# A rotary embedding on one core: how slab 0 is loaded, and how some loads and stores are cut into DMAs

## The chip, the cores and the metric

The kernel runs on one core of one Trainium2 chip. The metric is the device time of one execution in microseconds (us); several executions are timed and the median is given. One further execution is taken with the hardware profiler, and all views below come from it.

## What is computed

`x` is a float32 tensor of 16 batches, 512 positions and 1024 numbers (16 heads of 64). `cos` and `sin` have one row of 32 numbers for each position. In each head, the first 32 numbers x1 and the last 32 numbers x2 are turned against each other:

```python
x1, x2 = x[..., :half_dim], x[..., half_dim:]
rotated = np.concatenate([x1 * cos - x2 * sin,
                          x1 * sin + x2 * cos], axis=-1)
```

The output has the size of `x`: 33.55 MB are read and as many written, with very little arithmetic on each number.

## The kernel before

**Tiling.** The input is taken as 8 slabs of two batches (`nslabs` = 8), 4 MB each: 128 partitions with 8 positions each (`rpp` = 8), so 8192 numbers or 32 KB in a partition. Two slabs make a pair. The two slabs of a pair lie side by side in memory for each partition (line 60), so a DMA of one slab moves rows of 32 KB and a DMA of a pair moves rows of 64 KB. There are three tiles for pairs in the core's memory (line 52, `places`); the fourth pair (slabs 6 and 7) takes the place of the first.

**Loads and stores.** `load(s, n, parts)` and `store(s, n, parts)` (lines 68 to 73) move n slabs from slab s on, on the partitions `parts`. Both go through `issue` (line 65) on SP's DMA queue, in the order of the program. `EVEN` and `ODD` (line 76) are every second partition. The order on SP is: load 0 (line 79), load 1 (line 94), load 2-3 in an EVEN and an ODD part (lines 95 and 96), load 4-5 (line 97); then store 0-1 and load 6-7, each in an EVEN and an ODD part, when slab 1 is done (lines 174 to 177); store 2-3 as one DMA when slab 3 is done, store 4-5 in an EVEN and an ODD part when slab 5 is done, store 6-7 as one DMA when slab 7 is done (lines 178 to 180). Load 6-7 EVEN waits for store 0-1 EVEN, and the ODD part for the ODD part, since they use the same memory.

**ScalarE's queue** has three DMAs at the start: the two tables cos and sin (line 89, 64 partitions with 1 KB each), and a short write of a zeroed tile `blank` (128 numbers, 512 bytes, lines 82 and 83) to the first bytes of the output (line 91). Store 0-1 later overwrites these bytes.

**The tables.** GpSimd casts the tables to bf16 (line 112), TensorE spreads them over the 128 partitions by matmuls against a tile of ones and minus ones (line 119), and VectorE (table 0, line 126) and ScalarE (table 1, line 159) copy them out.

**The work on a slab.** It goes in passes: slab 0 in two passes of 4 positions, slab 7 in passes of 4, 2 and 2, all others in one (line 134). For each pass ScalarE casts the float32 slab to bf16 into the lower half of its own memory (`cast`, line 147), VectorE multiplies twice by a table (line 167) and adds (line 170), and ScalarE copies the result out as float32 over the slab (line 173). All ScalarE copies go through line 151, in the order of the program. In the round of slab s, ScalarE first casts slab s+1 (lines 161 to 164) and then copies slab s out, so a slab's copy-out, and the store behind it, stand behind the landing of the next slab.

**Semaphores.** The framework gives each DMA one of eight completion semaphores in turn. The ninth DMA takes the one of the first, and its issue waits until the first has landed.

Of the kernel before, what the change touches and what calls it, by code (L numbers as in the profile page):

```python
# [2 lines left out]

# [4 lines left out]


@with_exitstack  # L10
def kernel(
    ctx: ExitStack,
    tc: tile.TileContext,
    x: bass.AP,
    cos: bass.AP,
    sin: bass.AP,
    num_heads: int,
    out: bass.AP,
):
    nc = tc.nc  # L20
    P = nc.NUM_PARTITIONS

    batch, seq, dim = x.shape
    nh = num_heads
    hd = dim // nh
    half = hd // 2
    bf16 = mybir.dt.bfloat16
    f32 = mybir.dt.float32

    nb = 2  # L30
    nslabs = batch // nb
    rpp = nb * seq // P
    W = rpp * dim
    TP = seq // rpp
    TW = rpp * half

    out_flat = out.rearrange("b s h d -> b s (h d)")

    singles = ctx.enter_context(tc.tile_pool(name="singles", bufs=1))
    pairs = ctx.enter_context(tc.tile_pool(name="pairs", bufs=3))  # L40
    psum = ctx.enter_context(tc.tile_pool(
        name="psum", bufs=1, space=bass.MemoryType.PSUM))


    def view(t, offset, *dims):
        return dataclasses.replace(t, offset=t.offset + offset,
                                   ap=[t.ap[0], *[list(d) for d in dims]])

    places = [pairs.tile([P, 2 * W], f32, tag="pair", name="pair") for _ in range(3)]


    def here(s, n=1):
        return view(places[s // 2 % 3], s % 2 * W, (1, n * W))


    def there(t, s, n=1):
        return bass.AP(tensor=t.tensor, offset=t.offset + s // 2 * 2 * P * W + s % 2 * W,  # L60
                       ap=[[2 * W, P], [1, n * W]])


    def issue(out, in_):
        tc.keep_in_program_order(nc.sync.dma_start(out=out, in_=in_))  # L65


    def load(s, n=1, parts=slice(None)):
        issue(here(s, n)[parts], there(x, s, n)[parts])


    def store(s, n=1, parts=slice(None)):
        issue(there(out_flat, s, n)[parts], here(s, n)[parts])


    EVEN, ODD = slice(0, P, 2), slice(1, P, 2)


    load(0)


    blank = singles.tile([1, P], f32, tag="blank")
    nc.vector.memset(blank, 0.0)  # L83


    cos_sb = singles.tile([TP, TW], f32, tag="cos_sb")
    sin_sb = singles.tile([TP, TW], f32, tag="sin_sb")
    for t, src in ((cos_sb, cos), (sin_sb, sin)):
        tc.keep_in_program_order(nc.scalar.dma_start(out=t, in_=bass.AP(
            tensor=src.tensor, offset=src.offset, ap=[[TW, TP], [1, TW]])))  # L90
    tc.keep_in_program_order(nc.scalar.dma_start(out=bass.AP(
        tensor=out_flat.tensor, offset=out_flat.offset, ap=[[P, 1], [1, P]]), in_=blank))

    load(1)
    for parts in (EVEN, ODD):
        load(2, 2, parts)
    load(4, 2)


    pick = singles.tile([TP, 4 * P], bf16, tag="pick")  # L100
    nc.gpsimd.memset(pick, 0.0)  # L101
    for h in range(2):
        for g in range(2):
            part = view(pick, (2 * h + g) * P, (TP // 2, 2 * P // TP), (1, TP // 2))
            nc.gpsimd.affine_select(  # L105
                out=part, in_=part, compare_op=mybir.AluOpType.not_equal,
                fill=1.0 - 2.0 * g, base=-h, pattern=[[0, 2 * P // TP], [-2, TP // 2]],
                channel_multiplier=1)

    tab1 = singles.tile([TP, 2 * TW], bf16, tag="tab1")  # L110
    for i, t in enumerate((cos_sb, sin_sb)):
        nc.gpsimd.tensor_copy(out=view(tab1, i * TW, (1, TW)), in_=t)  # L112

    accs, tabs = [], []
    for h in range(2):
        acc = psum.tile([P, 2 * rpp * hd], f32, tag=f"acc{h}", name="acc")
        for i in range(2):
            for f in range(2):
                nc.tensor.matmul(  # L119
                    view(acc, i * rpp * hd + f * half, (hd, rpp), (1, half)),  # L120
                    view(pick, (2 * h + i * f) * P, (1, P)),
                    view(tab1, i * TW, (half, rpp), (1, half)),
                    start=True, stop=True)
        accs.append(acc)
        tabs.append(singles.tile([P, 2 * rpp * hd], bf16, tag=f"tab{h}", name="tab"))
    nc.vector.tensor_copy(out=tabs[0], in_=accs[0])  # L126

    passes = []
    for s in range(nslabs):
        r = 0
        for n in {0: (4, 4), nslabs - 1: (4, 2, 2)}.get(s, (rpp,)):
            passes.append((s, r, n))
            r += n


    def halves(u):
        s, r, n = u  # L140
        t = here(s).bitcast(bf16)
        return [view(t, (2 * r + i * n) * dim, (1, n * dim)) for i in range(2)]


    def cast(u):
        s, r, n = u
        copy(halves(u)[0], view(here(s), r * dim, (1, n * dim)))


    def copy(out, in_):  # L150
        tc.keep_in_program_order(nc.scalar.copy(out=out, in_=in_))  # L151


    for i, u in enumerate(passes):
        s, r, n = u
        if i == 0:
            cast(u)
            cast(passes[1])
            copy(tabs[1], accs[1])
            cast(passes[2])  # L160
        elif s > 0:
            for v in passes:
                if v[0] == s + 1:
                    cast(v)
        lo, up = halves(u)
        for t, a in ((up, 0), (lo, rpp * hd)):
            nc.vector.tensor_mul(  # L167
                out=t, in0=lo,
                in1=view(tabs[s % 2], a + r * hd, (hd, n), (0, nh), (1, hd)))
        nc.vector.tensor_add(  # L170
            out=up, in0=up, in1=view(lo, half, (hd, n * nh), (-half, 2), (1, half)))

        copy(view(here(s), r * dim, (1, n * dim)), up)
        if s == 1:
            for act in (store, load):
                for parts in (EVEN, ODD):
                    act(0 if act is store else 6, 2, parts)
        elif s % 2 and r + n == rpp:
            for parts in (EVEN, ODD) if s == 5 else (slice(None),):
                store(s - 1, 2, parts)  # L180


# [1 line left out]
_INS = ['x', 'cos', 'sin', 'num_heads']  # L184
_OUTS = [((16, 512, 16, 64), 'float32')]

_NUMBERS = {'num_heads': 16}


# [26 lines left out]
```

## Time and profile before

| what | us |
|---|---|
| median of 3 executions (161.56 to 162.01) | 161.57 |
| the profiled execution | 161.8 |
| its span, from first to last instruction | 160.0 |
| ScalarE (ACT) busy | 114.0 |
| VectorE (DVE) busy | 108.0 |
| GpSimd (POOL) busy | 2.6 |
| TensorE (PE) busy | 2.0 |

All times in the views are counted from the first instruction of the span. These moments of the profiled execution come up later. They are landings of DMAs and the times at which SP issues a DMA:

| event | at us |
|---|---|
| SP issues load 0 | 0.74 |
| cos lands, sin lands | 10.84, 16.11 |
| load 0 lands, first cast on ScalarE | 13.59, 13.61 |
| first multiply on VectorE | 18.56 |
| load 1 lands | 23.40 |
| load 2-3 has landed (the ODD part) | 42.75 |
| SP issues store 0-1 | 56.80 |
| load 4-5 lands | 62.23 |
| load 6-7 has landed | 101.02 |
| SP issues store 6-7 | 137.66 |
| store 6-7 lands | 159.19 |

A group of instructions in the profile is given by line, engine, operation and tile; "<-DMA pair<-in_x_dram" behind an idle time says what ended it. "q1" is SP's DMA queue and "q10" ScalarE's. One DMA is cut into packets, here one for each partition's row, and these are shared out over 16 DMA engines; each engine also writes a record of 4 bytes when its part of a DMA is complete.

### The profile page before, as it was taken

What the parts mean: (1) busy time and instruction counts of PE and PEld (TensorE: products, weight loads), DVE (VectorE), ACT (ScalarE), POOL (GpSimd) and SP (SyncE); (2) the same over time, 40 slices, a digit from 0 to 9 for tenths busy, and PEclk for the clock granted to TensorE, in tenths of its full rate; (3) what the DMA queues carried; (4) which work ended last, traced back from release to release, by engine and by line L of the source; (5) the groups of instructions that cost most, each with busy time, mean ns of one, the idle gap of its engine ahead of it and who ended that gap; (6) DMA issues with size and microseconds to landing.
All of it is one profiled execution on the core that took longest, in us unless ns stands there. A gap on an engine that the chain in (4) does not pass through costs nothing.

```text
span 160.0 us, 176 instructions
## 1 busy us (share of the span) xinstructions
PE 2.0 (1%) x8; PEld 1.0 (1%) x8; DVE 108.0 (68%) x35; ACT 114.0 (71%) x24; POOL 2.6 (2%) x11
## 2 busy tenths in 40 slices
PE   0010300000000000000000000000000000000000
PEld 0000100000000000000000000000000000000000
DVE  0000699999935998999899899919999997000000
ACT  3005959993299999999999995799999969400000
POOL 4000000000000000000000000000000000000000
DMA  7999999699699699897996996996996996996991
GB/s 262 405 401 405 393 524 524 262 524 524 262 524 524 262 524 410 377 524 344 442 524 278 508 524 278 508 524 262 524 524 262 524 491 295 524 491 295 524 459 66
DMA packets 1522, 67.24 MB, mean 420 GB/s; under 512 B 241, under 2 KB 370, under 8 KB 370
## 3 DMA queue, kind: packets, MB, share of 16 engines
q1 hardware_dynamic: 1360, 67.11, 97.7%
q10 hardware_dynamic: 162, 0.13, 0.3%
HBM read 33.69 MB, written 33.55 MB: 420 GB/s over the span
## 4 chain that ended last, share of the span: by engine, by line
DMA 53%; DVE 14%; ACT 12%; issue 5%; ACTq 2%; SPq 1%
DMA pair<-in_x_dram 37%; DMA out_dram<-pair 15%; ACT pair L151 12%; DVE pair L167 10%; DVE pair L170 4%; ACTq L211 1%; SPq L65 1%; ACTq L151 0%
## 5 line engine op out<-in xcount | busy, mean ns | idle before, releaser
L151 ACT CAST pair<-pair 128x8192 bf16<-128x8192 f32 (+5 forms) x22 | 111.8, 5153 | 20.9 <-DMA pair<-in_x_dram 19.5
L167 DVE TENSOR_TENSOR pair<-pair,tab 128x8192 bf16<-128x8192 bf16 (+2 forms) x22 | 71.4, 3259 | 9.8 <-ACT pair L151 9.4
L170 DVE TENSOR_TENSOR pair<-pair 128x8192 bf16<-128x8192 bf16 (+2 forms) x11 | 35.8, 3259 | 0.3
L126 DVE CAST tab<-acc 128x1024 bf16<-128x1024 f32 x1 | 1.2, 1225 | 16.2 <-PE acc L119 16.2
L151 ACT ACT_TABLE_LOAD x1 | 1.3, 1283 | 2.8 <-issue 2.8
L119 PE MATMUL acc<-tab,pick 64*128 64x256 bf16 x8 | 2.0, 405 | 16.0 <-POOL tab L112 16.0
L119 PEld LDWEIGHTS <-pick 64*128 64x128 bf16 x8 | 1.0, 130 | 16.5 <-issue 14.5
L105 POOL TENSOR_SCALAR_AFFINE_SELECT pick<-pick 64x128 bf16<-64x128 bf16 x4 | 1.1, 302 | 0.1
L151 ACT CAST tab<-acc 128x1024 bf16<-128x1024 f32 x1 | 1.0, 1003 | 0.0
L83 DVE MEMSET blank<- 1x128 f32 x1 | 0.2, 165 | 0.8 <-PEq L197 0.8
L112 POOL CAST tab<-cos_sb 64x256 bf16<-64x256 f32 x1 | 0.4, 389 | 8.5 <-DMA cos_sb<-in_cos_dram 8.5
L101 POOL MEMSET pick<- 64x512 bf16 x1 | 0.5, 517 | 0.3 <-POOLq L197 0.3
L112 POOL CAST tab<-sin_sb 64x256 bf16<-64x256 f32 x1 | 0.4, 394 | 4.9 <-DMA sin_sb<-in_sin_dram 4.9
L197 POOL MEMSET const-float32-0.0<- 128x1 f32 x1 | 0.1, 103 | 0.2 <-issue 0.2
L197 POOL MEMSET const-bfloat16-1.0<- 128x1 bf16 x1 | 0.1, 106 | 0.0
L197 POOL MEMSET const-uint8-127<- 128x1 uint8 x1 | 0.1, 106 | 0.0
L197 POOL MEMSET const-float32-1.0<- 128x1 f32 x1 | 0.1, 103 | 0.0
## 6 DMA issues: line engine op xcount, KB each, us to landing
pair<-in_x_dram SPq DMA_DIRECT2D x2, 4096.0 KB, 17.5
out_dram<-pair SPq DMA_DIRECT2D x6, 22.8
pair<-in_x_dram SPq DMA_DIRECT2D x5, 36.0
cos_sb<-in_cos_dram ACTq DMA_DIRECT2D x1, 64.0 KB, 10.1
sin_sb<-in_sin_dram ACTq DMA_DIRECT2D x1, 64.0 KB, 14.8
out_dram<-blank ACTq DMA_DIRECT2D x1, 0.5 KB
```

The lines of the kernel that those rows point to most:

```text
L65: tc.keep_in_program_order(nc.sync.dma_start(out=out, in_=in_))
L83: nc.vector.memset(blank, 0.0)
L101: nc.gpsimd.memset(pick, 0.0)
L105: nc.gpsimd.affine_select(out=part, in_=part, compare_op=mybir.AluOpType.not_equal, fill=1.0 - 2.0 * g, base=-h, pattern=[[0, 2 * P // TP] ...
L112: nc.gpsimd.tensor_copy(out=view(tab1, i * TW, (1, TW)), in_=t)
L119: nc.tensor.matmul(view(acc, i * rpp * hd + f * half, (hd, rpp), (1, half)), view(pick, (2 * h + i * f) * P, (1, P)), view(tab1, i * TW, ( ...
L126: nc.vector.tensor_copy(out=tabs[0], in_=accs[0])
L151: tc.keep_in_program_order(nc.scalar.copy(out=out, in_=in_))
L167: nc.vector.tensor_mul(out=t, in0=lo, in1=view(tabs[s % 2], a + r * hd, (hd, n), (0, nh), (1, hd)))
L170: nc.vector.tensor_add(out=up, in0=up, in1=view(lo, half, (hd, n * nh), (-half, 2), (1, half)))
L197: nc = _bacc.Bacc("TRN2", target_bir_lowering=False, num_devices=1)
L211: with _tile.TileContext(nc) as tc:
```

## The change

Slab 0 is loaded by four DMAs, the k-th of which takes the partitions k, k+4, k+8 and so on (32 partitions each). The `blank` tile, its memset and its write to the output are gone. Load 2-3 and store 4-5 are one DMA over all partitions instead of an EVEN and an ODD part. Store 0-1 and load 6-7 stay cut in two.

```diff
-    load(0)
-
-
-    blank = singles.tile([1, P], f32, tag="blank")
-    nc.vector.memset(blank, 0.0)
+    for k in range(4):
+        load(0, 1, slice(k, P, 4))
...
-    tc.keep_in_program_order(nc.scalar.dma_start(out=bass.AP(
-        tensor=out_flat.tensor, offset=out_flat.offset, ap=[[P, 1], [1, P]]), in_=blank))
 
     load(1)
-    for parts in (EVEN, ODD):
-        load(2, 2, parts)
+    load(2, 2)
     load(4, 2)
...
         elif s % 2 and r + n == rpp:
-            for parts in (EVEN, ODD) if s == 5 else (slice(None),):
-                store(s - 1, 2, parts)
+            store(s - 1, 2)
```

In the compiled program the number of DMAs on SP stays 13. Two waits stand elsewhere than before. SP's issue of load 4-5, now the ninth DMA, waits for the first one by the order of the semaphores, which is cos. And ScalarE's waits for slab 0, now four, are spread over two instructions: three of them stand on the load of the activation table, which is the instruction ahead of the first cast, and one on the cast.

## The prediction

> **What bounds the kernel now.** I read the page from its DMA rows first, because two engines are busy only some 70% of the span and neither leads. These are lines of the page: the span, the DMA rows of the 40 slices, and the load queue.
>
> ```profile
> span 160.0 us, 176 instructions
> ...
> DMA  7999999699699699897996996996996996996991
> GB/s 262 405 401 405 393 524 524 262 524 524 262 524 524 262 524 410 377 524 344 442 524 278 508 524 278 508 524 262 524 524 262 524 491 295 524 491 295 524 459 66
> ...
> q1 hardware_dynamic: 1360, 67.11, 97.7%
> ```
>
> The 16 engines spend 97.7% of the span on SP's queue. The dips to 262 GB/s look like idling, but each stands beside 524: a slice is 4 us, and long packets are counted where they begin. Stretches cut at the landings (the view of busy time in windows; the last two columns are DMA share and GB/s) even this out:
>
> ```profile
> 0.00:2.00 2.00, 0.00 (x0) 0.10 (x1) 0.17 (x1) 0.00 (x0) 1.40 (x8) 1.00 0.68 197
> 2.00:23.40 21.40, 2.02 (x8) 0.94 (x7) 6.04 (x4) 9.30 (x4) 1.19 (x4) 1.00 1.03 429
> 23.40:61.50 38.10, 0.00 (x0) 0.00 (x0) 33.41 (x10) 32.70 (x6) 0.00 (x0) 1.00 0.97 420
> 61.50:81.00 19.50, 0.00 (x0) 0.00 (x0) 18.43 (x5) 19.50 (x4) 0.00 (x0) 1.00 1.06 457
> 81.00:100.50 19.50, 0.00 (x0) 0.00 (x0) 18.87 (x6) 17.29 (x3) 0.00 (x0) 1.00 1.01 437
> 100.50:139.00 38.50, 0.00 (x0) 0.00 (x0) 31.12 (x13) 35.17 (x9) 0.00 (x0) 1.00 0.99 427
> 139.00:160.00 21.00, 0.00 (x0) 0.00 (x0) 0.00 (x0) 0.00 (x0) 0.00 (x0) 1.00 0.86 371
> ```
>
> No stretch between 2.0 and 139 us is below 0.97. The trace also holds a record of every DMA packet (queue, start, duration, size), and these say it sharply: each engine moves 16 packets of 32 KB and 56 of 64 KB. A 64 KB packet takes 2.418 us, a 32 KB packet 1.213, each starting as the last ends. So the packets alone need 16 x 1.213 + 56 x 2.418 = 154.8 us; the first starts at 1.76 us and the last ends at 158.85, 157.1 us later. The loss is 2.3 us in all: 0.53 because the first packet of an engine takes 1.74 (median), 0.45 in the nine packets after about 8 us, some 0.5 where a store follows a load or the last store begins, the rest in 162 short packets, in how far the engines start apart (1.76 to 2.31) and in how far they end apart (157.96 to 158.85). **The queue is never empty.** Only what shortens or lengthens this row of packets, or lets it run dry, moves the end.
>
> Does it nearly run dry? The waits of SP's queue and the longest waits of the compute engines:
>
> ```profile
> SPq L65 <- ACT pair L151: 91.5, 4, 38.5
> SPq L65 <- DMA out_dram<-pair: 23.4, 2, 13.9
> ...
> SPq L65 <- DMA out_dram<-blank: 4.6, 1, 4.6
> ```
>
> ```profile
> 42.83 20.86 ACT L151 CAST pair<-pair 128x8192 bf16<-128x8192 f32 x3 [5.37 <-DMA pair<-in_x_dram]
> ```
>
> SP issues a store when ScalarE's last copy of a pair is done. By the packet records the queue had work until 61.3 when store 0-1 was issued at 56.8, until 119.3 when store 4-5 was issued at 116.8, and until 138.6 (first engine) to 139.3 (last) when store 6-7 was issued at 137.66. Issue to first packet is at most 1.0 us there, so the slack is about 3.5, 1.5 and 0 to 0.7 us. The last two count from slab 6-7's landing at 101.02: chain and queue both hang on it and shift together, so a shift of the whole row keeps this slack.
>
> **The change, part by part.** All against the profiled execution: 161.8 us, of which 160.0 is the span and 1.8 lies around it; the median of the runs is 161.57, 0.23 lower.
>
> 1. *Slab 0 in four DMAs.* Bytes, row length (32 KB) and packet count are the same: 32 partitions over 16 engines, two packets each, four times. Three more completion records per engine at 9 ns each: +0.03 us. SP issues four instead of one; the issues of this line took 0.39 to 0.60 us, so the fourth is out near 2.5 us, when each engine is still on the first two packets (3.0 us of work from 1.76). Not starved. Does a stride of 4 cost? No trace shows it; the nearest row is a stride of 2: the EVEN and ODD loads of slabs 2-3 took 2.42 us per packet, like load 4-5 over all partitions. I take 0. Bounds: below, the short list may reach the late engines earlier (they start up to 0.55 after the first) and spare the slow first packet (0.53), together -1.1; above, +1.6 (rival C).
>
> 2. *Tables land earlier.* The engine takes a packet of SP's queue and one of ScalarE's in turn. Now cos has five turns (four packets of 46 ns and the completion) and sin five more, each behind a 1.21 us packet, so they land at 10.84 and 16.11. Afterwards the quarters' completions take turns of 9 ns, so cos ends after the fourth x packet instead of the sixth and sin after the eighth instead of the tenth: about 8.2 and 13.2 us. It would let VectorE's first multiply (18.56 now, 2.45 after sin) start at 15.7.
>
> ```profile
> 13.61 7.11 ACT L151 CAST pair<-pair 128x4096 bf16<-128x4096 f32 x2 [9.55 <-DMA pair<-in_x_dram]
> 16.17 0.39 POOL L112 CAST tab<-sin_sb 64x256 bf16<-64x256 f32 x1 [4.89 <-DMA sin_sb<-in_sin_dram]
> ```
>
> But it needs ScalarE's first cast too, and that moves the other way. In the changed program the waits for three quarters hang on the activation table load ahead of that cast, the last quarter's among them. That load (1.28 us, from 2.78 now) then runs at about 13.7 to 15.0, and the first cast from 15.0 to 18.6, as late as VectorE starts today. Queued behind it on ScalarE: the second cast (3.6) and the copy of table 1 (1.0), done at 23.1, still before slab 1 lands (23.4; 1.79 us of idle time there now pays for the 1.28). Sum 0. If this cover were gone, VectorE's idle 4.5 us ahead of 49.88, waiting for slabs 2-3 (42.75), hides up to 4.5 us more. An earlier multiply is worth nothing for the same reason.
>
> 3. *Load 4-5 waits.* The changed program makes SP wait for the cos DMA before it issues load 4-5 (it is the ninth DMA, and reuses that one's semaphore). Behind it on SP stands store 0-1, due at 56.8. Load 4-5 goes out near 8.2 us instead of 3; the queue has work till 41.9. Cost 0, cover 33 us.
>
> 4. *Load 2-3 and store 4-5 whole.* One issue (about 0.5 us of SP) and one completion record per engine less each: -0.02 us. ScalarE waits for both halves of slabs 2-3 today anyway; packets of half and whole stores both take 2.418 us. Cost 0; bounds 0.3 both ways from the 0.1 to 0.34 us by which single packets at a change from load to store are longer.
>
> 5. *No short write.* It goes with VectorE's memset (0.17), one issue on ScalarE (0.79, in its idle time), a 27 ns packet with its completion on one engine, and the 4.6 us that SP waits for its landing, which lie inside the wait for 56.8. Gain 0.04 at most. Above: +0.5 (rival D).
>
> Sum: +0.03 - 0.02 - 0.04, and about -0.1 for a slightly earlier and closer start: 161.8 - 0.1 = 161.7 profiled, 161.5 beside the median.
>
> **The rivals.**
>
> B, *the start gains more*: short lists start all 16 engines together and the slow first packet shrinks. For: the last three engines start 0.1 us after one another. Against: engines that start late today finish their first packet in 1.47 to 1.64 instead of 1.8 to 2.0, so that the starts' spread of 0.55 is already 0.47 at its end, and the four engines that end last are not these three. 0.5 to 1.1 less: about 160.8.
>
> C, *each quarter starts cold* (the other side): the second to fourth quarter pays the 0.53 us of a first packet again, 3 x 0.53 = +1.6, 163.1. It decides once a quarter's first packet is over 0.16 us (a third of 0.48) longer than 1.213, since nothing behind slab 0 gives time back. Against: load 1 follows load 0 in the same queue with 1.3 us packets amid sin's, and loads 2-3 follow with no step at all. [...]
>
> D, *the short write warms the path to the output*: without it the first store's packets pay what the first load's did, +0.5, 162.1. For: all first store packets take 2.418 us today, with no slow first one. Against: it ran on one engine of 16, and the other 15 are as fast.
>
> E, *the change does more than the row of packets shows*, through the earlier tables: excluded up to 4.5 us by VectorE's wait, so it has no share of its own.
>
> **How the numbers follow.** About 0.3% (0.48 us) is what a measurement here can tell from no change. Forecast, no change, 161.5 (161.1 to 162.0): 0.72, of which 0.03 passes the bound on either side. B 0.13, C 0.07, D 0.08, half of it past the bound. Faster 0.13 + 0.03 = 0.16; slower 0.07 + 0.04 + 0.03 = 0.14; same 0.70. The range 160.9 to 162.1 takes in the forecast, about half of B and most of D.
>
> **What would show it.** Right: x packets at 1.21 and 2.42 us with no gap; cos landing near 8.2 and sin near 13.2; the table load at 13.7 and the first multiply within 0.5 us of 18.56; store 0-1 issued near 56.8 and store 6-7 near 137.6; 97 to 98% on q1. Wrong: 32 KB packets well over 1.3 us in the quarters (C); the first packets of the first store over 2.5 us (D); a last store issued over 1 us after the queue ran dry; or slabs 2-3 landing before 42.3 (B).

## The result and the profile after

| | before | changed |
|---|---|---|
| median of 22 runs each, us | 161.88 (161.47 to 162.37) | 162.24 (161.84 to 162.63) |
| ratio to before | 1 | 1.0020 (95%: 1.0011 to 1.0030) |
| profiled execution, its span, us | 161.8, 160.0 | 162.38, 160.6 |

The change costs 0.36 us. That is inside the 0.3% that was named as the bound of "no change", but it has the other sign than the forecast, and 162.24 lies above the range that ended at 162.1. Of the 0.74 us between the forecast and this median, 0.31 belong to the yardstick: the three runs of the kernel before had a median of 161.57, the 22 runs of it beside the changed kernel 161.88. The same 0.36 us on top of 161.57 would have been 161.93, inside the range. So three runs were too few to forecast a time to 0.3 us, and that much of the miss is bad luck; the sign of the change is not.

One correction to the section on the change: SP issues 14 DMAs in the changed kernel, not 13. With the tables (and the short write, before) there are 16 in all in both kernels. This number comes up again.

The page of the changed kernel, the lines that answer to those of before:

```profile
span 160.6 us, 176 instructions
...
DMA  5999999699699697996996996997998998989974
GB/s 171 399 458 441 392 522 522 261 522 522 261 522 506 278 522 310 473 522 261 522 522 261 522 522 261 522 441 343 522 424 359 522 424 359 522 375 408 522 343 180
...
q1 hardware_dynamic: 1376, 67.11, 97.5%
```

The queue is as full as before (97.5% against 97.7%). What differs is the first digit: 5 instead of 7. The windows at the start say the same (the last columns are DMA share and GB/s):

```profile
0.00:2.00 2.00, 0.00 (x0) 0.10 (x1) 0.00 (x0) 0.00 (x0) 1.41 (x8) 1.00 0.00 0
2.00:23.40 21.40, 2.02 (x8) 0.93 (x7) 5.61 (x3) 9.30 (x4) 1.18 (x4) 1.00 1.08 447
```

In the first 2 us, where the kernel before had a share of 0.68, no packet has begun. The chain of the first microseconds shows what SP does there (start, duration), first before, then changed:

```profile
0.74 0.39 SPq L65
1.13 0.05 issue
1.18 0.42 SPq L65
1.61 0.04 issue
1.65 0.57 SPq L65
```

```profile
0.73 0.55 SPq L65
1.28 0.06 issue
1.34 0.58 SPq L65
```

These issues of a DMA over all partitions take 0.39 to 0.42 us, those of every fourth partition 0.55 to 0.58. A DMA that takes every second or every fourth partition is called stepped below. The second issue ends at 1.60 before and at 1.91 now. By the packet records the first packet begins 0.16 us after that in both: at 1.76 and at 2.08. The 0.57 in the chain of before is the EVEN part of load 2-3, and a whole load 2-3 took 0.42 at the same place (kernels 3 and 7 below): the price of a stepped issue stood in the view of before. From the fourth issue on the step no longer tells: load 4-5, over all partitions, took 0.60 before.

Then the timeline of slab 0 in the changed kernel:

```profile
11.59 0.39 POOL L106 CAST tab<-sin_sb 64x256 bf16<-64x256 f32 x1 [4.62 <-DMA sin_sb<-in_sin_dram]
...
14.05 1.28 ACT L145 ACT_TABLE_LOAD   x1 [14.05 <-DMA pair<-in_x_dram]
15.34 7.11 ACT L145 CAST pair<-pair 128x4096 bf16<-128x4096 f32 x2
18.98 6.82 DVE L161 TENSOR_TENSOR pair<-pair,tab 128x4096 bf16<-128x4096 bf16 x3 [5.10 <-ACT pair L145]
```

The tables land at 6.52 and 11.53 (before: 10.84 and 16.11), the table load waits for slab 0, and VectorE starts 0.42 us later than before, now waiting for ScalarE. Nothing follows from that: VectorE still idles 4.31 us ahead of slab 2. Store 0-1 is issued at 57.00 (56.80), store 6-7 at 138.30 (137.69 by its record; 137.66 in the table of before).

### The profile page after: what moved, and what is told of

Its sections match the earlier page's. It is cut to its first block, busy times and chain, and to the rows that moved or that the text cites. A ratio compares the mean times of both kernels' runs of the same rounds, so it can differ in the third digit from the quotient of the medians.

```text
span 160.6 us, 176 instructions
## 1 busy us (share of the span) xinstructions
PE 2.0 (1%) x8; PEld 1.0 (1%) x8; DVE 107.9 (67%) x34; ACT 114.0 (71%) x24; POOL 2.6 (2%) x11
## 3 DMA queue, kind: packets, MB, share of 16 engines
q1 hardware_dynamic: 1376, 67.11, 97.5%
## 4 chain that ended last, share of the span: by engine, by line
DMA 52%; DVE 14%; ACT 12%; issue 5%; SPq 2%; ACTq 2%
DMA pair<-in_x_dram 36%; DMA out_dram<-pair 15%; ACT pair L145 12%; DVE pair L161 10%; DVE pair L164 4%; SPq L65 2%; ACTq L204 1%; ACTq L145 0%
```

## How the experiments were read

Packet records carry most of what follows, so here is one table of all profiles. "DMAs" counts those of both queues. "First" is the start of the first x packet; "load 1" the mean over the 16 engines of the end of its last packet; "joint" the mean duration of the last packets of load 4-5, those just ahead of the first store (2.418 without a joint); "last" the mean end of the last packets; "tail" the time from the last landing to the end of the span. Several values are several profiles of one kernel.

| kernel | DMAs | first | load 1 | joint | last | tail | ratio to before (95%) |
|---|---|---|---|---|---|---|---|
| before | 16 | 1.76, 1.76 | 22.73, 22.79 | 2.58, 2.67 | 158.31, 158.57 | 0.83, 0.83 | |
| load 1 late | 16 | 1.76 | 22.71 | 2.62 | 158.37 | 0.83 | |
| tables late | 16 | 1.75 | 22.77 | 2.61 | 158.32 | 0.83 | 1.0000 (0.9988 to 1.0012) |
| write on 16 engines | 16 | 1.76 | 22.75 | 2.60 | 158.33 | 0.83 | 1.0009 (1.0000 to 1.0017) |
| no write | 15 | 1.75 | 22.69 | 2.65 | 158.32 | 0.90 | 1.0007 (0.9997 to 1.0017) |
| 2-3, 4-5 whole | 14 | 1.76 | 22.68 | 2.86 | 158.73 | 0.96 | 1.0006 (0.9998 to 1.0014) |
| store 0-1, load 6-7 whole | 14 | 1.76 | 22.75 | 2.85 | 162.05 | 0.96 | (one run) |
| changed, slab 0 whole | 13 | 1.74, 1.74 | 22.97, 22.78 | 2.43, 2.75 | 158.46, 158.46 | 1.02, 1.02 | 1.0021 (1.0011 to 1.0031), 1.0012 (1.0001 to 1.0023) |
| changed | 16 | 2.08, 2.06, 2.07 | 22.93, 22.99, 23.09 | 2.86, 2.84, 2.53 | 159.06, 158.87, 158.63 | 0.83, 0.83, 0.83 | 1.0020 (1.0011 to 1.0030), 1.0017 (1.0007 to 1.0027) |
| changed, with write | 17 | 2.06 | 23.03 | 2.66 | 158.61 | 0.93 | 1.0028 (1.0017 to 1.0039) |
| halves | 17 | 2.34 | 22.94 | 3.08 | 159.18 | 0.94 | 1.0041 (1.0026 to 1.0056) |
| quarters, 2-3 whole | 18 | 2.35 | 22.92 | 3.00 | 158.91 | 1.00 | 1.0051 (1.0035 to 1.0067) |
| quarters, no write | 18 | 2.35, 2.35 | 22.97, 22.95 | 3.31, 2.97 | 159.27, 158.87 | 1.00, 1.00 | 1.0052 (1.0038 to 1.0066) |
| quarters alone | 19 | 2.35 | 23.01 | 3.17 | 159.16 | 1.06 | 1.0064 (1.0040 to 1.0088) |
| blocks | 16 | 1.77 | 32.51 | 2.42 | 167.96 | 0.83 | 1.0592 (1.0578 to 1.0606) |

The theory after the result was: the loss has two places, the start (stepped issues) and the joint ahead of the first store (the missing short write). Its rivals: one of the two alone, the cuts of load 2-3 and store 4-5, or scatter.

## The experiments

**1. Quarters alone.**

```diff
-    load(0)
+    for k in range(4):
+        load(0, 1, slice(k, P, 4))
```

> The kernel before with slab 0 alone cut into four DMAs. Theory (two places: the start pays for the cut, the first store pays for the missing short write): first packets start near 2.08 us instead of 1.76, load 1 lands about 0.25 later (23.65), the last packets of load 4-5 stay at a median of 2.55 us as before, and the end is 0.2 to 0.3 us later than before. Rival (the start costs nothing in the end, all of the loss is at the first store): the same landing of load 1 shift, but the end within 0.1 us of before. Second rival (the longer packets at the first store come from the cut of slab 0): last packets of load 4-5 near 2.9 us, end +0.4 to +0.6.

162.66 against 161.81, 0.85 us: more than the whole change (one of the eight runs took 164.21, hence the wide interval). The first packets are at 2.35 and the joint is 3.17, longer even than the second rival had it; the theory, with 2.08 and 2.55, is wrong in both. Against the means of four profiles (16 names them), this one has lost 0.26 us at the end of load 1, 0.55 in the joint and 0.23 in the tail; 16 says what the tail is.

**2. No short write.**

```diff
-    blank = singles.tile([1, P], f32, tag="blank")
-    nc.vector.memset(blank, 0.0)
...
-    tc.keep_in_program_order(nc.scalar.dma_start(out=bass.AP(
-        tensor=out_flat.tensor, offset=out_flat.offset, ap=[[P, 1], [1, P]]), in_=blank))
```

> The kernel before without the short write and its tile. Theory: the first packets start at 1.76 us and load 1 lands at 23.4 as before; the last packets of load 4-5, those before the first store, take a median of 2.9 us instead of 2.55 and the end is 0.2 to 0.4 us later. Rival (these packets scatter from execution to execution or depend on how loads and stores are cut): 2.5 to 2.6 us, end within 0.1 us of before.

Joint 2.65, 161.85 against 161.81: the rival. Leaving out the write shows nowhere; the first store's packets take 2.418 us here too.

**3. Load 2-3 and store 4-5 whole.**

```diff
-    for parts in (EVEN, ODD):
-        load(2, 2, parts)
+    load(2, 2)
...
-            for parts in (EVEN, ODD) if s == 5 else (slice(None),):
-                store(s - 1, 2, parts)
+            store(s - 1, 2)
```

> The kernel before with load 2-3 and store 4-5 as one DMA each. Theory: no change, end within 0.1 us of before, and the last packets of load 4-5 at 2.5 to 2.6 us. Rival (the cut of load 2-3 sets how the first store begins): last packets of load 4-5 near 2.9 us and the end 0.2 to 0.4 us later. A rise at the last store alone (its first packets over 2.45 us) would come from store 4-5 being whole, worth at most 0.1.

161.81 against 161.81, ratio 1.0006 with 1 in its interval. The joint was 2.86 in the one profile, as the rival had it, and that execution took 162.21, the longest of the 12; the median did not follow. So a long joint can belong to one execution and not to the kernel.

**4. The write on all 16 engines.**

```diff
-    blank = singles.tile([1, P], f32, tag="blank")
+    blank = singles.tile([16, P], f32, tag="blank")
...
-        tensor=out_flat.tensor, offset=out_flat.offset, ap=[[P, 1], [1, P]]), in_=blank))
+        tensor=out_flat.tensor, offset=out_flat.offset, ap=[[P, 16], [1, P]]), in_=blank))
```

> The kernel before with the short write widened from 1 row of 512 bytes to 16 rows, one for each of the 16 DMA engines. Theory (a first write to the output costs something on each engine, which the short write takes on itself where it runs): the last packets of load 4-5 fall from a median of 2.55 us toward 2.42 and the end is 0.05 to 0.3 us earlier. Rival (one early write does all there is to do, or the write does nothing): packets stay at 2.5 to 2.6 us, end within 0.1 us of before.

Joint 2.60, 162.02 against 161.81: nothing gained. A first write on every engine did not shorten the joint, against the theory of a warmed path.

**5. Quarters without the write, load 2-3 and store 4-5 still cut** (the edits of 1 and 2).

> The kernel before with slab 0 in four DMAs and without the short write; load 2-3 and store 4-5 stay cut. The quarters alone cost 0.85 us with the short write in place (medians 162.66 and 161.81), and 0.36 in the whole change. Theory (two queues that issue at once hold each other up: ScalarE's short write at 2 us delays the lists of the quarters): without it first packets near 2.08 us and the end 0.3 to 0.4 us later than before. Rival (the uncut load 2-3 is what saves the rest): first packets near 2.35 as in the quarters alone, end 0.7 to 0.9 later.

162.56 against 161.75, first packets at 2.35: the rival, the write holds up nothing.

**6. The changed kernel with the write.**

```diff
+    blank = singles.tile([1, P], f32, tag="blank")
+    nc.vector.memset(blank, 0.0)
...
+    tc.keep_in_program_order(nc.scalar.dma_start(out=bass.AP(
+        tensor=out_flat.tensor, offset=out_flat.offset, ap=[[P, 1], [1, P]]), in_=blank))
```

> The changed kernel with the short write put back. Theory (the short write delays the quarters): first packets near 2.35 us and the end 0.7 to 0.9 us later than before. Rival (load 2-3 uncut saves the rest): first packets near 2.08 us, end 0.3 to 0.4 later.

First packets at 2.06, 162.20 against 161.75 (0.45): the rival again, a little beyond its 0.4. That it is load 2-3 that saves the rest is not shown by this; 14 tests it.

**7. The changed kernel with slab 0 whole.**

```diff
-    for k in range(4):
-        load(0, 1, slice(k, P, 4))
+    load(0)
```

> The changed kernel with slab 0 in one DMA again. Theory (all of the loss is from the quarters): first packets at 1.76 us, load 1 landing at 23.4, end within 0.15 us of before. Rival (leaving out the write or the cuts costs by itself): end 0.2 to 0.4 us later, with the last packets of load 4-5 at 2.9 us.

162.10 against 161.75 (0.35), though the first packets are at 1.74 and the joint is gone (2.43): neither. Load 1 ended at 22.97, as late as with quarters. By this the quarters would cost nothing; 16 takes it up.

**8. Blocks.**

```diff
-        load(0, 1, slice(k, P, 4))
+        load(0, 1, slice(32 * k, 32 * k + 32))
```

> The changed kernel with slab 0 cut into four blocks of 32 neighbouring partitions instead of every fourth partition. Theory (it is the number of DMAs that costs at the start): same as the changed kernel, packets of 1.21 us, end 0.2 to 0.5 us later than before. Rival (it is the stride of four partitions that makes the issue of each DMA longer): first issue 0.39 instead of 0.55 us, first packets at 1.8, end within 0.15 of before. [...]

171.28 against 161.75: neither. Windows of this kernel over slab 0 and over what follows:

```profile
2.00:22.00 20.00, 2.02 (x8) 0.94 (x7) 1.23 (x1) 0.00 (x0) 1.19 (x4) 1.00 0.95 198
22.00:42.00 20.00, 0.00 (x0) 0.00 (x0) 13.26 (x6) 17.92 (x6) 0.00 (x0) 1.00 1.00 423
```

The engines are busy (0.95) at half the rate: 198 GB/s against 423. Their eight packets of slab 0 cost 9.7 us more, and the end is 9.5 later, so next to nothing behind slab 0 gives time back. The quarters show no such loss: from 2.00 to 13.00 us, amid slab 0, the changed kernel has 393 GB/s and the kernel before 392. Why 32 neighbouring partitions load at this rate is not shown by the runs. The block's first issues, though, are short:

```profile
0.73 0.40 SPq L65
1.13 0.06 issue
1.19 0.41 SPq L65
```

and its first packet begins at 1.77. So it is the step and not the number of DMAs that makes the start late, and a DMA of 32 partitions sets out no sooner than one of 128.

**9 to 11. Second profiles** of the changed kernel, of kernel 5 and of before (no edit).

> The changed kernel once more, for a second profile. Theory (what the last packets of load 4-5 take, ahead of the first store, belongs to the kernel): their mean is 2.86 us again, within 0.1. Rival (it scatters from execution to execution): anything from 2.4 to 3.3 us. The start is steady in either: first packet at 2.08, 0.16 after SP's second issue ends.

> The kernel before with the four quarters and without the short write once more, for a second profile. Theory (the first store's delay belongs to the kernel): mean 3.3 us again for the last packets of load 4-5. Rival (scatter): 2.4 to 3.3 us. The start is steady in either: SP's second issue 0.8 us, first packet at 2.35.

> The kernel before once more, for a second profile. Theory (the first store's delay belongs to the kernel): 2.58 us again for the last packets of load 4-5, within 0.1. Rival (scatter): 2.4 to 3.3 us. First packet at 1.76 us in either.

The start repeats to 0.02 us. The joint repeats roughly: 2.84, 2.97 (3.31 first) and 2.67. It scatters by 0.1 to 0.3 within a kernel; the 2.97 and 3.31 still lie above both values of before. These three and the next are single executions (162.28, 162.38, 161.83 and 161.73 us, beside 162.16 for another one of before), so their times decide nothing.

**12. Load 1 late.**

```diff
+    nc.gpsimd.memset(view(places[0], W, (1, 512)), 0.0)
     load(1)
```

> The kernel before with a short memset by GpSimd on a part of slab 1's place, for which SP's second issue (load 1) waits; the memset's values are overwritten by the load. SP's second issue then begins at about 1.5 us instead of 1.18. Theory (the engines set out only when the second issue is through, by 0.16 us in ten profiles): first packets at 2.0 to 2.2 us instead of 1.76. Rival (the second issue is long because the first one's lists are still being made, and these alone decide): first packets stay at 1.76, and the second issue gets shorter instead.

The second issue began at 1.29 instead of 1.18 and took 0.34 instead of 0.42 us; the packets began at 1.76. That is as the rival had it, but the issue moved by 0.11 us where 0.3 was meant, and its end, at 1.63, by 0.03: the theory would have put the packets at 1.79. A difference of 0.03 us cannot tell the two apart, so whether the first packet waits for the second issue or both wait for something else stays open.

**13. Store 0-1 and load 6-7 whole.**

```diff
-            for act in (store, load):
-                for parts in (EVEN, ODD):
-                    act(0 if act is store else 6, 2, parts)
+            store(0, 2)
+            load(6, 2)
```

> The kernel before with store 0-1 and load 6-7 as one DMA each. Load 6-7 then waits for the whole store, so the queue runs dry for about 1.5 us after it and the end is 1 to 2 us later; what counts is the joint before the first store. Theory (the joint is longer because the first store is cut in two, so that two lists are made at once): last packets of load 4-5 near 2.45 us, as at the later joints, instead of 2.6. Rival (the cut has no part in it): 2.55 to 2.9 us.

Joint 2.85: the cut of the store has no part in it. The span is 163.7, 3.6 more: the queue ran dry from 81.45 to 82.77, the packets after that took 3.11 (median), and the next joint (load 6-7 to store 2-3) 3.49 instead of 2.47. More than the 1 to 2 us expected.

**14. Quarters with only load 2-3 whole** (1 and the first half of 3).

> The kernel before with slab 0 in four DMAs and load 2-3 as one; the short write and the cut of store 4-5 stay. Theory (a whole load 2-3 halves what the quarters cost): SP's second issue 0.57 us, first packets near 2.07, end 0.3 to 0.5 us later than before. Rival (the whole store 4-5 does it): second issue 0.82 us, first packets near 2.35, end 0.7 to 0.9 later.

162.71 against 161.82, first packets at 2.35: the rival. The long second issue (0.82 us) goes with a cut store 4-5: four kernels have both (quarters or halves, and the cut store), and the two stepped ones without it (the changed kernel and 6) take 0.57 to 0.58. Why a store at 115 us should lengthen an issue at 1.4 us stays open.

**15. Halves, and late tables.**

```diff
-    load(0)
+    for parts in (EVEN, ODD):
+        load(0, 1, parts)
```

> The kernel before with slab 0 in an EVEN and an ODD DMA. Theory (a step of partitions makes a DMA's issue and lists longer): first issue 0.55 instead of 0.39 us, first packets at 2.0 to 2.4 us and the end 0.2 to 0.6 us later than before. Rival (only the number of DMAs counts): first packets at 1.76, end within 0.15 us.

162.52 against 161.82 (0.70), with first packets at 2.34, as late as in 1, 5 and 14. The chain of this kernel:

```profile
0.73 0.58 SPq L65
1.31 0.06 issue
1.37 0.82 SPq L65
```

So a step of two is as dear as a step of four, with two DMAs instead of four. The other kernel holds ScalarE's table issues back:

```diff
+    nc.gpsimd.memset(cos_sb, 0.0)
     for t, src in ((cos_sb, cos), (sin_sb, sin)):
```

> The kernel before with a memset of the cos tile by GpSimd, for which ScalarE's first DMA issue waits (it goes out at about 1.2 us instead of 0.74; the load overwrites the memset). Theory (SP's lists alone set the start): first packets stay at 1.76 and the end within 0.15 us. Rival (the lists of both queues are made by one maker, so that cos holds slab 0 up): SP's second issue ends earlier, first packets at 1.4 to 1.6 us, and the end is 0.1 to 0.3 us earlier than before, which would beat both kernels.

Ratio 1.0000, first packets at 1.75 with cos issued at 1.07: ScalarE's issues do not hold SP's up.

**16. Slab 0 whole in the changed kernel, and the changed kernel, side by side** (no new edit).

> The changed kernel with slab 0 in one DMA, timed again. Theory (the rest of the change costs 0.35 by itself): 0.2 to 0.5 us slower than before again. In its profile slab 1 lands near 23.6 (0.25 after before), the packets amid the tables' being longer, and the last packets of load 4-5 take 2.43. Rival (the first timing was chance, the quarters cost it all): within 0.15 us of before and slab 1 at 23.4.

> The changed kernel, timed beside the one with slab 0 whole. Theory (the quarters cost nothing more within the change): equal to it within 0.15 us, 0.2 to 0.5 slower than before. Rival (the quarters cost it all): 0.3 to 0.5 slower than the one with slab 0 whole.

161.96 and 162.10 against 161.76. In this second profile of slab 0 whole, load 1 ended at 22.78 and the joint was 2.75, so neither the 22.97 nor the 2.43 of 7 belongs to the kernel. The quarters are worth 0.14 by the medians, which is not clear of the error: each interval is some 0.2% wide, 0.3 us. But the tails show what the rest is. SP ends the program by five wait instructions of two semaphores each, among them the eight of the DMAs; in the records one begins about 0.06 us after the other (138.09, 138.15, 138.21 before). With 16 DMAs the last store has the eighth semaphore, the last instruction waits for it, and the tail is 0.83. With 15, 14, 13 DMAs one, two, three instructions stand behind it: 0.90, 0.96, 1.02. With 17, 18, 19 the semaphores have begun anew, and two, three, four stand behind it: 0.93, 1.00, 1.06. Slab 0 whole in the changed kernel makes 13 DMAs, so this kernel pays 0.19 in its tail, and the changed kernel, with 16 again, pays nothing. Its packets end at 158.46 on the mean, 0.07 after those of the four profiles of before, of load 1 late and of the late tables (158.39); those of the changed kernel at 158.85, 0.46 after.

## Why the prediction was wrong, by its steps

**What bounds the kernel** held. In every profile but that of 13 the queue is full (97.3 to 97.8% on q1 in the pages of before, changed, 1, 8, halves and slab 0 whole), and blocks, halves and quarters show that what is lost by the end of load 1 is kept (9.7 us there and 9.5 at the end in the blocks): nothing on the engines gave it back.

**Step 1 failed**: "a slightly earlier and closer start", -0.1, and the stride of four at 0. The nearest row was taken for the packets alone (EVEN and ODD packets at 2.42, and indeed the quarters' packets behind the first take 1.21 to 1.35 on the mean of the engines, as before). The issue of a stepped DMA, 0.57 against 0.39 in the chain of before, was counted as SP's time. That time was free later on, where the queue had work (load 2-3 and store 4-5 cut or whole: a ratio of 1.0006 in 3), and not at the head of the queue: there the first packet came 0.32 us later behind two stepped issues, and not behind the unstepped ones of the blocks. The start is not closer either: the first packets of the 16 engines begin within 0.67 to 0.94 us of each other in the three profiles of the changed kernel, and within 0.49 to 0.77 in the four of before that 16 names. Measured: first packet +0.32, and +0.25 at the end of load 1 (22.75 on the mean of four profiles before, 23.00 of three after). The other 0.07 came back beside the tables, where fewer packets are lengthened (the 3rd to 6th of each engine instead of the 5th to 10th).

**Step 2** had the mechanism, not the sizes. Cos landed at 6.52 instead of 8.2: between the first two quarters an engine has no x packet for some 0.18 us, and the four cos packets go through in one gap. The table load waits at 14.05 (13.7 forecast), the first multiply comes at 18.98 (within the 0.5 named), and the cover was there as said.

**Step 3** held: SP waits for cos (2.1 us), then nothing.

**Steps 4 and 5** gave 0 and -0.04. Singly each is within its error of zero (1.0006, 1.0007); where they stand without the quarters, the tail is longer by 0.13 us for step 4 and 0.07 for step 5, by the count of DMAs, which the prediction did not look at. In the change itself the four quarters bring the count back to 16.

**Rivals.** B (the start gains) did not come: with the quarters the first packet of an engine takes 1.72 to 1.80 us on the mean (1.78 to 1.81 before) and begins later, and the blocks, as short, begin at 1.77 against 1.76. C had the right place and sign and the wrong mechanism: the later quarters start warm, at 1.21 to 1.35 us on the mean, with single packets up to 1.44 beside the tables. D did not show: without the write, in 2 and in the change, the first store's packets take 2.418 us.

**Two readings** in the prediction were off, and nothing in the sum hangs on them. Store 4-5 was issued at 115.06 and 115.61 us, not at 116.8, so it had more slack than 1.5. And of the three engines that start late, one took 1.73 us for its first packet; the others of the 16 took 1.64 to 2.04.

**The sum of the change**, from means of three and four profiles: start +0.25, joint ahead of the first store +0.12 (2.74 against 2.62), later joints and the last store +0.09 (in the first profile the last store's packets begin 0.12 after their engines ran dry; the slack of 0 was real), tail 0; 0.46 to 0.49 in the profiles, 0.36 and 0.34 between the medians of the two timings. Only the start is clear of the scatter between profiles (22.93 to 23.09 against 22.71 to 22.79; of slab 0 whole, in 7, one profile reached 22.97 without quarters and its second did not); the joint (2.53 to 2.86 against 2.58 to 2.67) and the later terms are not. **Open**: what sets the length of the joint between a load and a store. It ranged from 2.42 to 3.31 us ahead of the first store, is longest where slab 0 and store 4-5 are both cut, and showed no dependence on the short write or on the cut of store 0-1. Also open is why a stepped DMA takes longer to issue, and how much of the 0.36 us the quarters cause within the change: taking them out also moves the tail by 0.19, and the 0.14 that is left between the medians is not clear of the error.

None of the kernels beats the kernel before; late tables equal it.

## What to carry to other kernels

When the DMA queue is full from end to end, price an edit by the first packet, the joints and the closing waits, since here the packets in between cost the same, whole or stepped (2.42 us for 64 KB). Issue the very first DMAs without a step of partitions (with it the first packet came at 2.06 to 2.35 us instead of 1.76); a step was free only where the queue had a backlog (1.0006 in 3). Before cutting a tile by partitions, measure the rate of the pieces (8): blocks of 32 neighbours ran at 198 GB/s, every fourth partition at 393. And forecast from more than three runs where tenths of a microsecond count.

## What was not expected of the hardware

- The first packet starts 0.13 to 0.17 us after the end of SP's second DMA issue in every profile, at 1.74 to 2.35 us; a stepped first DMA made it late by 0.3 or 0.6 (2.06 to 2.08, or 2.34 to 2.35, against 1.76).
- In these profiles a load followed by a store cost 0 to 0.9 us in the last packets of the load ahead of the first store (2.42 to 3.31 instead of 2.418), and 1.07 at one later joint (in 13); a store followed by a load cost nothing where the queue did not run dry (2.418).
- After the queue ran dry for 1.3 us (in 13), the next 64 KB packets took 3.11 instead of 2.418 us, longer like the first packets of the program (1.74 instead of 1.213).
- The program ends with five wait instructions in turn, 0.06 us apart; the place of the last store's semaphore among them moved the end by up to 0.23 us (tails of 0.83 to 1.06).
